# Scores of a banded attention as three products of split parts in place of one plain float32 product

## The chip, the cores and the metric

One Trainium2 chip, one core. The metric is the device time of one execution in microseconds; a kernel's time is the median of its runs.

## What is computed

The kernel computes two transformer-like blocks of two layers each, one after the other, on 256 tokens of width 1024. The change lies in the first block. Each of its layers has three branches: a state-space branch, a banded attention with rotated queries and keys (the one that changes), and a full attention with decay. Cut to the banded attention:

```python
def sliding_window_branch(q, k, v, z, sinks, cos, sin):
    q = rope(q.reshape(b, s, SWA_HEADS, HEAD_DIM), cos, sin)       # 16 heads of 64
    k = rope(k.reshape(b, s, SWA_KV_HEADS, HEAD_DIM), cos, sin)    # 4 heads of 64
    ...
    scores = einsum('bnqkgd,bnskd->bnkgqs', qb, kb) * HEAD_DIM ** -0.5   # blocks of 128, this block and the one before
    scores = where(band & (key_pos >= 0), scores, -inf)
    probs = softmax(concat([scores, sink], -1))[..., :-1]
    out = einsum('bnkgqs,bnskd->bnqkgd', probs, vb)
    return out.reshape(b, s, SWA_HEADS * HEAD_DIM) * silu(z)
```

All inputs are float32.

## The kernel before

Activations lie with features on the partitions and tokens on the columns. A dense unit (`dense`, line 287) multiplies 1024 by 256 weights with 256 tokens: 8 steps over the contraction, two blocks of 128 outputs, and three products each (`mm3`, line 245). Both operands are split: a rounded copy in float32r (ScalarE, `act`) and the rest (a VectorE or GpSimd subtraction, `tt`), and high x high, high x low and low x high are summed in PSUM. The weights come by DMA into `wr`, are copied to `wh` by ScalarE and their rest `wl` is made by VectorE, for one piece in four by GpSimd (`fetch`, line 115), for a unit two ahead of the one that is used.

The attention's own products (scores, transposes, probabilities times values) are plain float32 matmuls, with no split.

The order on TensorE is written out by hand: the program text is the order. Small work is woven between the dense units by a clock of its own: `spent` counts the columns streamed and calls `tick` every 3072, a half step; a dense unit is 2 steps. Tasks (`spawn`) are Python generators that yield the number of steps until they go on. A `Job` is one pair of heads: A makes scores and softmax, B, at least 2.5 steps later, the transposes, C the product with the values. The order on the other engines is made by the scheduler, which also inserts the waits.

In a layer of the first block, the banded attention comes after the full attention. First the keys' dense unit: ScalarE reads it out to `swk`, `rope` (line 775) starts four DMAs on ScalarE's queue that swap halves of 32 partitions into a scratch tile `s`, and a task follows: 2 steps later `s` is multiplied on GpSimd and the keys on VectorE, one step later VectorE adds the two. Then the values' unit. Then four rounds, one for each four query heads (loop at line 802): a dense unit for the queries, read out with the scale to `q`, `rope(q)`; a dense unit for the gate `z`; the two jobs are enqueued, 2 steps later at the earliest and after `turned` and `kturned` have ended; a dense unit for the merge gate and one that projects the other attention's output (`gate_proj`, line 758). `qk` (line 234) makes the scores: for the pair's two heads, which lie on partitions 0 to 63 and 64 to 127, first block by first keys (128 columns), then second block by all keys (256 columns). With 2 layers, 4 rounds and 2 pairs it runs 16 times for this attention, and as often for the full one, which keeps it.

Scratch tiles (`f2`, 2 KB a partition) come from a pool of 13 buffers in this block. In the trace all scratch tiles are named f, the scores' PSUM tiles ps, dense PSUM tiles pd, transposes pt, the product with the values po; line numbers are those of helpers (L92 `mm`, L98 `act`, L101 `tt`, L104 `stt`).

Of the kernel before, what the change touches and what calls it, by code (L numbers as in the profile page):

```python
# [6 lines left out]
F32 = mybir.dt.float32  # L7
F32R = mybir.dt.float32r
# [3 lines left out]
ALU = mybir.AluOpType  # L12
# [33 lines left out]
class Kern:  # L46
# [187 lines left out]
    def qk(self, pss, cuts, q, k):  # L234

        for a, b, c, d in cuts:
            for i, ps in enumerate(pss):
                p = slice(64 * i, 64 * i + 64)
                self.mm(ps[:, a:b], q[p, 128 * (a > 0):128 * (a > 0) + 128], k[p, c:d], True, True)

    def masked(self, out, ps, mask, least, init=3e38):

        self.V.tensor_tensor_reduce(out, ps, mask, 1.0, init, ALU.add, ALU.min, least)  # L243
# [266 lines left out]
def b1_layer(K, l, x, yr, sums, cw, wdt, first_sums=None):  # L510
# [112 lines left out]
    def gate_z(ps):  # L623
        zs = K.f2((128, 2, 256))
        K.act(zs, ps, AF.Tanh, scale=0.5)
        K.stt(zs, zs, 1.0, ps, ALU.add, ALU.mult)
        return zs
# [6 lines left out]
    def pv2(o, pair, v, pts):  # L634
        for i in range(2):
            K.mm(o[64 * i:64 * i + 64, pair, :], v(i, 0), pts[i][0], True, False)
        for i in range(2):
            K.mm(o[64 * i:64 * i + 64, pair, 128:256], v(i, 1), pts[i][1], False, True)

    def attn4(score, v, masks, mn_fix, done, wait=0, until=(), row0=None):  # L640


# [4 lines left out]
        def job(pair):  # L647
# [6 lines left out]
            def A():  # L654
                add = sh.get("b")
                mn = K.small([128, 2, 2], "mn")
                pss = [K.psx((128, 384)) for _ in range(2)]
                score(pair, pss)
                sh["p"] = prs = []
                if mn_fix is not None:  # L660
                    ns, sk = mn_fix(pair)
                for i, ps in enumerate(pss):
                    pr = add[i] if add else K.f2((128, 384))
                    for a, s in enumerate((slice(0, 128), slice(128, 384))):
                        K.masked(pr[:, s], ps[:, s], pr[:, s] if add else masks[a], mn[:, i, a:a + 1],
                                 3e38 if mn_fix is None else ns[:, i:i + 1])
                    prs.append(pr)
                den = K.small([128, 2, 2], "den")
                if mn_fix is not None:
                    es = K.small([128, 2, 2], "es")  # L670
                    K.tt(es, mn, sk, ALU.add)
                    K.act(es, es, AF.Exp)
                for i, pr in enumerate(prs):
                    for a, s in enumerate((slice(0, 128), slice(128, 384))):
                        K.act(pr[:, s], pr[:, s], AF.Exp, scale=-1.0, bias=mn[:, i, a:a + 1],
                              accum_out=den[:, i, a:a + 1])
                if mn_fix is not None:
                    K.tt(den, den, es, ALU.add)
                V.reciprocal(den, den)
                for i in range(2):  # L680
                    pr = prs[i]
                    V.tensor_scalar(pr[:, 0:128], pr[:, 0:128], den[:, i, 0:1], None, op0=ALU.mult)
                    V.tensor_scalar(pr[:, 128:384], pr[:, 128:384], den[:, i, 1:2], None, op0=ALU.mult)
# [27 lines left out]
    def gated(yt, zs, c0):  # L711
        def done(o):
            t = K.f2((128, 2, 256))
            K.stt(t, o, 0.5, zs, ALU.mult, ALU.mult)
            split_y(yt, t, c0)
        return done
# [4 lines left out]
    for i in range(4):  # L721
        q, kk, v = [K.f2((128, 2, 256)) for _ in range(3)]
        if i == 0:
            ps = K.dense(K.unit(), Hr, (0, 1))
# [23 lines left out]
        def score(pair, pss, q=q, kk=kk, i=i):  # L748
            K.qk(pss, ((0, 128, 0, 128), (128, 384, 0, 256)), q[:, pair, :], kk[:, pair, :])

        jc += attn4(score, lambda j, t, v=v: v[:, t, 64 * j:64 * j + 64], None, None, gated(yc, zs, 2 * i),
                    until=(steps,), row0=64 + 4 * i)

# [4 lines left out]
    def gate_proj(br, y, i, jobs, first):  # L758
        Y = (lambda k: y[:, 0, k, :], lambda k: y[:, 1, k, :])
        ps = K.dense(K.unit(), H, (0, 1))  # L760
        th = K.f2((128, 2, 256))
        for c in range(2):
            f = 8 * br + 2 * i + c
            K.act(th[:, c, :], ps[:, c, :], AF.Tanh, scale=0.5, bias=gbh[:, f:f + 1])
        K.finish_jobs(jobs)
        ps = K.dense(K.unit(), Y, (0, 1))
        m = merged[:, 2 * i:2 * i + 2, :]
        if first:
            K.stt(m, th, 1.0, ps, ALU.add, ALU.mult)
        else:  # L770
            K.stt(th, th, 1.0, ps, ALU.add, ALU.mult)
            K.tt(m, m, th, ALU.add, K.P)


    def rope(t):
        s = K.f2((128, 2, 256))
        for a in range(4):
            b = a ^ 1
            nc.scalar.dma_start(s[32 * a:32 * a + 32], t[32 * b:32 * b + 32])

        def task():
            yield 2
            K.tt(s, s, K.bc(K.rope[:, 1, :], 2), ALU.mult, K.P)
            K.tt(t, t, K.bc(K.rope[:, 0, :], 2), ALU.mult)
            yield 1
            K.tt(t, t, s, ALU.add)

        turned = K.spawn(task())
        K.step(turned)
        return turned  # L790

    ps = K.dense(K.unit(), H, (0, 1))
    kk = K.k_p.tile([128, 2, 256], F32, name="swk", tag="k0")
    K.act(kk, ps)
    kturned = rope(kk)
    ps = K.dense_tok(K.unit(), H)
    v = K.k_p.tile([128, 2, 256], F32, name="swv", tag="k1")
    K.act(v, ps)
    yb = K.r_p.tile([128, 2, NK, 256], F32R, name="yb", tag="r16")
    nsk = K.small([128, 16], "nsk")  # L800
# [1 line left out]
    for i in range(4):  # L802
        g0 = 2 * (i // 2)
        ps = K.dense(K.unit(), H, (0, 1))
        q = K.f2((128, 2, 256))
        K.act(q, ps, scale=-0.125)
        turned = rope(q)
        zs = gate_z(K.dense(K.unit(), H, (0, 1)))

        def score(pair, pss, q=q, i=i):  # L810
            K.qk(pss, ((0, 128, 0, 128), (128, 384, 0, 256)), q[:, pair, :], kk[:, i // 2, :])

        def fix(pair, i=i):
            s = slice(4 * i + 2 * pair, 4 * i + 2 * pair + 2)
            return (nsk[:, s],
                    vec("sink", 16 * l, 16)[:, s].unsqueeze(2).to_broadcast([128, 2, 2]))

        js = attn4(score, lambda j, t, g0=g0: v[:, t, 64 * (g0 + j % 2):64 * (g0 + j % 2) + 64],
                   (K.msk("u"), K.msk("le", 2)), fix, gated(yb, zs, 2 * i), 2, (turned, kturned))
        jb += js  # L820
        gate_proj(2, yc, i, jc, True)
# [92 lines left out]
    for i in range(4):  # L914
        ps = K.dense(K.unit(), H, (0, 1))
# [8 lines left out]
    for i in range(4):  # L924
        th = pend[i]
        w = K.unit()
        for cols in ((0,), (1,)) if i == 3 else ((0, 1),):
            ps = K.dense(w, Y, cols)
# [640 lines left out]
def program(tc, A, out, dbg=None):  # L1569
    with ExitStack() as ctx:  # L1570
# [14 lines left out]
        with ExitStack() as c1:  # L1585
# [49 lines left out]

            mods = K.spawn(later(), 5)
            mg = b1_layer(K, 0, x1, yr, sums, cw[0], wdt, first_sums)
            sums = K.sums_open(K.gather)
            yr = raw()
# [6 lines left out]

            b1_out(K, 0, x1, mg, sums, None, None, between)
            mg = b1_layer(K, 1, x1, yr, sums, cw[1], wdt)
            K.finish(mods)

# [297 lines left out]
```

## Time and profile before

| | us |
|---|---|
| median of 3 runs | 2063.96 |
| lowest and highest | 2060.04 and 2064.75 |
| the profiled execution's own time | 2062.68 |
| its span, first to last instruction | 2060.9 |
| TensorE matmuls busy | 2029.2 |
| VectorE, ScalarE, GpSimd busy | 1464.4, 991.1, 506.2 |

The profile is of one execution. PE is TensorE's matmul queue and PEld its weight loads, DVE is VectorE, ACT ScalarE, POOL GpSimd. Matmuls are pipelined: a row's duration reaches from the start of the first to the modelled end of the last, and so rows overlap; the distance between starts is what a matmul costs. float32r operands are shown as f32 in the matmuls' rows.

### The profile page before, as it was taken

The page shows a single profiled execution, that of the slowest core. Times are in us where ns is not written, and L with a number is a line of the kernel's source. Part 1 is how long each engine was busy: PE and PEld are TensorE (multiplying, and loading weights), DVE is VectorE, ACT ScalarE, POOL GpSimd, SP SyncE. Part 2 cuts the span into 40 slices and gives each one's busy share as a digit, 9 for nine tenths or more (in the row PEclk, how much of TensorE's full clock was granted, in tenths as well). Part 3 has the DMA queues.
Part 4 walks back from the last instruction along what each step waited for, and adds up shares of the span by engine and source line. Part 5 has one row for each costly group of instructions (what it writes and reads, how often), then busy time and mean ns, then how long its engine had stood idle before and what let it go on. Part 6 is the DMA issues. An engine that isn't in the chain of part 4 may idle for free.

```text
span 2060.9 us, 37605 instructions
## 1 busy us (share of the span) xinstructions
PE 2029.2 (98%) x14768; PEld 1839.0 (89%) x14768; DVE 1464.4 (71%) x2835; ACT 991.1 (48%) x2112; POOL 506.2 (25%) x393
## 2 busy tenths in 40 slices
PE   8999999999999999999999999999999999999998
PEld 7898999999898999999877888888888899999997
DVE  7777788976777788978466454865564576879984
ACT  6455555545455555555344333542332354556553
POOL 3232222324333123343100212111111121232222
PEclk9999999999999999999999999999999999999999
DMA  7765656665765656654111232232222233454552
GB/s 272 292 214 191 219 207 248 222 246 203 259 208 195 233 202 243 231 191 162 59 57 57 87 123 102 83 102 94 91 103 92 92 128 118 144 195 164 182 192 77
DMA packets 66304, 339.08 MB, mean 165 GB/s; under 512 B 7760, under 2 KB 22096, under 8 KB 29776
## 3 DMA queue, kind: packets, MB, share of 16 engines
q1 hardware_dynamic: 62000, 332.22, 45.7%
q10 hardware_dynamic: 4128, 4.46, 0.8%
q8 instruction: 116, 1.90, 0.4%
q14 instruction: 60, 0.49, 0.1%
HBM read 331.28 MB, written 1.44 MB: 161 GB/s over the span
## 4 chain that ended last, share of the span: by engine, by line
PE 92%; DVE 5%; issue 1%; ACT 1%; DMA 1%; SPq 0%; POOL 0%; DVEq 0%; POOLq 0%; ACTq 0%
PE pd L92 81%; PE ps L92 4%; PE po L92 3%; PE pt L92 2%; PE pt L95 2%; DVE wl L101 2%; DVE f L104 1%; DVE f L101 1%; ACT wh L98 0%; DMA wm<-in_wm_dram 0%; DVE h L104 0%; DMA x<-in_x_dram 0%; DVE f L984 0%; DVE hl L101 0%; ACT f L98 0%
## 5 line engine op out<-in xcount | busy, mean ns | idle before, releaser
L101 DVE TENSOR_TENSOR wl<-wr,wh 128x512 fp32r<-128x512 f32 x751 | 687.9, 934 | 244.7 <-ACT wh L98 243.1
L98 ACT ACTIVATE wh<-wr 128x512 fp32r<-128x512 f32 x992 | 561.2, 621 | 470.1 <-PE pd L92 262.1
L101 POOL TENSOR_TENSOR wl<-wr,wh 128x512 fp32r<-128x512 f32 x241 | 349.9, 1452 | 1238.9 <-ACT wh L98 1103.0
L92 PE MATMUL pd<-h,wh 128*128 128x256 f32 x2688 | 498.7, 286 | 2.4 <-ACT wh L98 1.4
L92 PEld LDWEIGHTS pd<-h,wh 128*128 128x128 f32 x2688 | 417.5, 191 | 26.4 <-issue 17.6
L92 PE MATMUL pd<-h,wl 128*128 128x256 f32 x1344 | 380.0, 283 | 0.7 <-DVE wl L101 0.7
L92 PE MATMUL pd<-hh,wh 128*128 128x512 f32 (+1 forms) x992 | 347.6, 350 | 1.5 <-ACT hh L98 1.5
L92 PE MATMUL pd<-hl,wh 128*128 128x512 f32 (+1 forms) x992 | 341.4, 344 | 3.7 <-DVE hl L101 3.7
L92 PE MATMUL pd<-hh,wl 128*128 128x512 f32 (+1 forms) x992 | 340.4, 343 | 0.0
L92 PEld LDWEIGHTS pd<-h,wl 128*128 128x128 f32 x1344 | 257.2, 191 | 1.2 <-DVE wl L101 0.9
L92 PEld LDWEIGHTS pd<-hh,wh 128*128 128x128 f32 x992 | 189.9, 191 | 30.4 <-issue 7.5
L92 PEld LDWEIGHTS pd<-hl,wh 128*128 128x128 f32 x992 | 190.1, 192 | 25.5 <-DVE hl L101 4.7
L92 PEld LDWEIGHTS pd<-hh,wl 128*128 128x128 f32 x992 | 190.0, 192 | 21.6
L92 PE MATMUL pd<-act,wh 128*128 128x256 f32 (+1 forms) x688 | 160.2, 327 | 0.0
L104 DVE SCALAR_TENSOR_TENSOR f<-pd,cw,f 128x255 f32<-128x255 f32 (+3 forms) x272 | 151.0, 555 | 11.0 <-ACT f L98 8.6
L92 PEld LDWEIGHTS pd<-act,wh 128*128 128x128 f32 x688 | 116.2, 190 | 11.1 <-DVE act L101 0.2
L92 PE MATMUL pd<-hf,wh 128*128 128x256 f32 x640 | 115.2, 283 | 0.0
L92 PE MATMUL pd<-mg,wh 128*128 128x256 f32 (+1 forms) x576 | 113.0, 296 | 0.1
L92 PE MATMUL pd<-act,wl 128*128 128x256 f32 (+1 forms) x344 | 112.2, 326 | 0.0
L98 ACT ACTIVATE f<-f,mn 128x128 f32<-128x128 f32 (+2 forms) x160 | 79.8, 500 | 46.8 <-DVE mn L243 46.6
L98 ACT ACTIVATE f<-pd,cw 128x256 f32<-128x256 f32 (+1 forms) x120 | 66.8, 557 | 69.6 <-DVE f L104 62.7
L92 PEld LDWEIGHTS pd<-hf,wh 128*128 128x128 f32 x640 | 99.8, 192 | 0.0
(257 smaller groups left out, 3216.5 us busy)
## 6 DMA issues: line engine op xcount, KB each, us to landing
wr<-in_w_dram SPq DMA_DIRECT2D x233, 1024.0 KB, 4.9
wm<-in_wm_dram SPq DMA_DIRECT2D x48, 1024.0 KB, 6.9
f<-far SPq DMA_DIRECT2D x32, 192.0 KB, 5.1
f<-far SPq DMA_DIRECT2D x24, 256.0 KB, 6.0
wr<-in_wd_dram SPq DMA_DIRECT2D x8, 768.0 KB, 4.2
wr<-in_wa_dram SPq DMA_DIRECT2D x8, 512.0 KB, 3.5
c<-in_c_dram SPq DMA_DIRECT2D x2, 1920.0 KB, 7.8
f<-f ACTq DMA_DIRECT2D x32, 64.0 KB, 2.0
```

Source lines behind the costliest of these rows:

```text
L92: self.T.matmul(out, l, r, start=start, stop=stop)
L95: self.T.transpose(out, in_, self.ident[0:k, 0:k])
L98: self.S.activation(out, in_, f, **kw)
L101: (eng or self.V).tensor_tensor(out, a, b, op=op)
L104: self.V.scalar_tensor_tensor(out, a, s, b, op0=op0, op1=op1)
```

## The change

`rope` is handed two tiles more. After the addition that ends the rotation, ScalarE copies the rotated tile to the first in float32r, and VectorE subtracts that copy from it into the second. The keys' two parts become `swk0` and `swk1` in the persistent buffers k0 and k1, the unsplit keys a scratch tile, and the values move to buffer k2. Each round's queries get two scratch tiles more. The scores are made by a new function `qk3`: for each of the two cuts three products, high x high, high x low, low x high, each for both heads in turn, summed in PSUM. Nothing else changes.

```diff
+    def qk3(self, pss, cuts, q, k):
+
+        (qh, ql), (kh, kl) = q, k
+        for a, b, c, d in cuts:
+            t = slice(128 * (a > 0), 128 * (a > 0) + 128)
+            for n, (x, y) in enumerate(((qh, kh), (qh, kl), (ql, kh))):
+                for i, ps in enumerate(pss):
+                    p = slice(64 * i, 64 * i + 64)
+                    self.mm(ps[:, a:b], x[p, t], y[p, c:d], n == 0, n == 2)
...
-    def rope(t):
+    def rope(t, parts):
...
             K.tt(t, t, s, ALU.add)
+            K.act(parts[0], t)
+            K.tt(parts[1], t, parts[0].bitcast(F32), ALU.subtract)
...
-    kk = K.k_p.tile([128, 2, 256], F32, name="swk", tag="k0")
-    K.act(kk, ps)
-    kturned = rope(kk)
+    kk = [K.k_p.tile([128, 2, 256], F32R, name="swk%d" % n, tag="k%d" % n) for n in range(2)]
+    kf = K.f2((128, 2, 256))
+    K.act(kf, ps)
+    kturned = rope(kf, kk)
     ps = K.dense_tok(K.unit(), H)
-    v = K.k_p.tile([128, 2, 256], F32, name="swv", tag="k1")
+    v = K.k_p.tile([128, 2, 256], F32, name="swv", tag="k2")
...
         K.act(q, ps, scale=-0.125)
-        turned = rope(q)
+        qs = [K.f2((128, 2, 256), F32R) for _ in range(2)]
+        turned = rope(q, qs)
...
-        def score(pair, pss, q=q, i=i):
-            K.qk(pss, ((0, 128, 0, 128), (128, 384, 0, 256)), q[:, pair, :], kk[:, i // 2, :])
+        def score(pair, pss, q=qs, i=i):
+            K.qk3(pss, ((0, 128, 0, 128), (128, 384, 0, 256)), [t[:, pair, :] for t in q],
+                 [t[:, i // 2, :] for t in kk])
```

## Rows read from the trace of the kernel before

**Rows 1.** The page: busy time by engine; the chain that ended last by engine.

```profile
PE 2029.2 (98%) x14768; PEld 1839.0 (89%) x14768; DVE 1464.4 (71%) x2835; ACT 991.1 (48%) x2112; POOL 506.2 (25%) x393
PE 92%; DVE 5%; issue 1%; ACT 1%; DMA 1%; SPq 0%; POOL 0%; DVEq 0%; POOLq 0%; ACTq 0%
```

**Rows 2.** Busy time by engine, both banded stretches together (139 to 275, 610 to 750).

```profile
sum 276.00, PE 274.65 PEld 248.03 DVE 207.23 ACT 150.88 POOL 70.98; mean PE 137.33 PEld 124.02 DVE 103.61 ACT 75.44 POOL 35.49
```

**Rows 3.** The banded scores by tile: count, duration in ns (min/median/max), starts, forms.

```profile
L92 PEld LDWEIGHTS ps<-swk,f x128: 182/188/188, 170.9 to 742.7; 64*128 64x128 f32 x128
L92 PE MATMUL ps<-swk,f x128: 272/375/378, 170.9 to 742.9; 64*128 64x128 f32 x64, 64*128 64x256 f32 x64
```

**Rows 4.** Timeline (start, us, engine, out<-in, count) of one unit, in narrow windows.

```profile
199.04 0.52 PEld L92 LDWEIGHTS ps<-swk,f 64*128 64x128 f32 x8
199.05 0.49 PE L92 MATMUL ps<-swk,f 64*128 64x128 f32 x4
199.37 0.60 PE L92 MATMUL ps<-swk,f 64*128 64x256 f32 x4
199.90 0.38 PE L92 MATMUL pd<-yc,wh 128*128 128x256 f32 x1
```

**Rows 5.** Timeline of TensorE inside a dense unit.

```profile
198.24 0.40 PE L92 MATMUL pd<-h,wh 128*128 128x256 f32 x2
198.48 0.28 PE L92 MATMUL pd<-h,wl 128*128 128x256 f32 x1
```

**Rows 6.** Timeline of all engines where an attention output is split.

```profile
150.54 0.68 DVE L104 SCALAR_TENSOR_TENSOR f<-po,f 128x512 f32<-128x512 f32 x1
...
151.25 0.63 ACT L98 ACTIVATE yc<-f 128x512 fp32r<-128x512 f32 x1 [3.12 <-DVE f L104]
...
151.92 0.69 DVE L101 TENSOR_TENSOR yc<-f,yc 128x512 fp32r<-128x512 f32 x1
```

**Rows 7.** Timeline of VectorE, second round of layer 0: product, addition, what follows.

```profile
191.71 1.76 DVE L101 TENSOR_TENSOR f<-f,rope 128x512 f32<-128x512 f32 x1
...
198.09 0.68 DVE L101 TENSOR_TENSOR f<-f,f 128x512 f32<-128x512 f32 x1
199.75 0.69 DVE L101 TENSOR_TENSOR wl<-wr,wh 128x512 fp32r<-128x512 f32 x1 [0.98 <-ACT wh L98]
```

**Rows 8.** Timeline of five more rounds: the addition, then the round's first scores.

```profile
228.01 0.68 DVE L101 TENSOR_TENSOR f<-f,f 128x512 f32<-128x512 f32 x1
...
229.13 0.93 PE L92 MATMUL ps<-swk,f 64*128 64x128 f32 x8
...
258.14 0.68 DVE L101 TENSOR_TENSOR f<-f,f 128x512 f32<-128x512 f32 x1
...
259.18 0.93 PE L92 MATMUL ps<-swk,f 64*128 64x128 f32 x8
...
670.16 0.68 DVE L101 TENSOR_TENSOR f<-f,f 128x512 f32<-128x512 f32 x1
...
673.33 0.93 PE L92 MATMUL ps<-swk,f 64*128 64x128 f32 x8
...
700.58 0.68 DVE L101 TENSOR_TENSOR f<-f,f 128x512 f32<-128x512 f32 x1
...
701.37 0.93 PE L92 MATMUL ps<-swk,f 64*128 64x128 f32 x8
...
730.33 0.68 DVE L101 TENSOR_TENSOR f<-f,f 128x512 f32<-128x512 f32 x1
...
731.45 0.93 PE L92 MATMUL ps<-swk,f 64*128 64x128 f32 x8
```

**Rows 9.** Timeline of ScalarE, second round of layer 0: its next weight copies.

```profile
199.09 2.19 ACT L98 ACTIVATE wh<-wr 128x512 fp32r<-128x512 f32 x4 [2.05 <-PE pd L92]
```

**Rows 10.** Timeline in layer 1: the keys' addition; the transposes that TensorE waits to start.

```profile
620.41 0.69 DVE L101 TENSOR_TENSOR swk<-swk,f 128x512 f32<-128x512 f32 x1 [1.82 <-POOL f L101]
...
622.56 0.97 PE L95 MATMUL pt<-cst,f 128*128 128x128 f32 x6 [1.35 <-DVE f L683]
```

## Prediction

> **What bounds the kernel now.** I read the page's engine line and chain first [rows 1]: TensorE's matmuls are busy 98% of the span and carry 92% of the chain of work that ended last, while VectorE is busy 71% and ScalarE 48%. So work saved on TensorE comes back one for one, and work given to the other engines is free as long as no matmul waits for it. Then the busy time of the two stretches that hold the banded attention (136 us in layer 0, 140 us in layer 1) [rows 2]: 274.7 of 276.0 us on TensorE, 207.2 on VectorE, 150.9 on ScalarE. TensorE has no gap there to hide anything in. Last the timelines around the scores, for which order on which engine decides what the matmuls wait for.
>
> **The scores on TensorE.** The group of the scores' matmuls counts 128 [rows 3]. The program has 2 layers x 4 rounds x 2 pairs x 2 cuts x 2 heads = 64, so each plain float32 product is issued as two instructions. One unit (one call for one pair: 8 instructions, 16 units in all) can be taken apart [rows 3, 4]. The two heads use different halves of the rows and start together: 8 weight loads of 0.19 fit in 0.52 us, so four pairs of loads stand 0.11 us apart ((0.52 - 0.19) / 3). The pairs of matmuls start at 199.05, 199.27 (0.49 - 0.27 later), 199.37 and 199.59 (0.60 - 0.38 later), and the next dense matmul at 199.90. Read as steps: first load 0.11, two narrow halves (128 columns) of 0.11, two wide ones (256) of 0.22, and a tail of 0.09 until the array turns to the next shape. Sum 0.86 (0.85 between the rows' starts).
>
> After the change a unit is 12 products with one instruction each, as the dense units have it, in six pairs: three narrow, three wide. A wide one: the dense 128x256 product of rounded parts has a pitch of 0.12 (two take 0.40, one 0.28) [rows 5]. A narrow product of rounded parts does not occur in this trace, so it is bounded. From below 0.06, half a wide one, if only columns count. From above 0.22, the two halves that a plain narrow product takes, if the rounded format gains nothing on so few columns. I take 0.11: each product needs its own weight load, and loads of exactly this shape stand 0.11 apart [rows 4]; that is the nearest row. A unit is then 0.11 + 3 x 0.11 + 3 x 0.12 + 0.09 = 0.89, against 0.86: +0.03, over 16 units **+0.5 us** (bounds: 0.74 gives -1.9, 1.22 gives +5.8). The half pass that three products save against four is eaten by the loads of the narrow ones.
>
> The rows put the narrow pace at the load's 0.11. The Trainium skill, page "TensorE: Matmul & The Clock Gate", section "LDWEIGHTS (loading the stationary operand)", says the same against this change: a load costs its 128 columns however few rows it has. The section "Back-to-back issue gap" of that page also has an isolated gap of N/2.4 + 2.5 ns, 56 ns for 128 columns, which leaves the load out and by which, as an estimate, the units would save some 2 us in place of adding 0.5; it warns itself that this counts too little for small N.
>
> **The split of the queries.** Each round of four heads gets a ScalarE copy to rounded form and a VectorE subtraction behind the rope's last addition, on queries that the next scores need. The same three steps stand in the trace where an output is split: VectorE ends at 150.54 + 0.68 = 151.22, ScalarE copies from 151.25 for 0.63, VectorE subtracts from 151.92 for 0.69 and ends at 152.61 [rows 6]. So the low part is there 1.39 us after the addition; with 0.03 to TensorE, 1.42. The high part is there after 0.69.
>
> Is there that much room? In the second round of layer 0 the addition stands behind a queue on VectorE: it runs 198.09 to 198.77, though the product before it ended at 191.71 + 1.76 = 193.47 [rows 7]. The scores start at 199.05 [rows 4], right after the tail of the dense unit, so nothing is waited for now, but the room is 0.28 us. The other rounds, addition's end to the scores [rows 8]: 0.44 and 0.36 in layer 0; 2.49, 0.11 and 0.44 in layer 1. The first rounds have several us, as their scores queue behind the other attention's jobs. TensorE's order is written out by hand, so a late part holds everything behind the scores: the next dense unit and the weight splits that wait for its buffers.
>
> The low queries are the third of the six pairs, whose load would start 0.22 after the first. The stall is 1.42 - 0.22 - room = 1.20 - room: 0.92, 0.76 and 0.84 in layer 0, none at room 2.49, 1.09 and 0.76 in layer 1: **+4.4 us**. For this the new steps must run at once. ScalarE is idle there, its next weight copies start at 199.09 after 2.05 idle [rows 9], and VectorE is idle for 0.98 until 199.75 [rows 7]; there is the place, if the scheduler's order puts the copy ahead of those four weight copies (2.19 us) and the subtraction ahead of their subtractions.
>
> **The split of the keys.** One per layer, needed by the first scores, two dense units later. In layer 1 the keys' addition (620.41, ends 621.10) stands directly ahead of VectorE's normalisation of the other attention, for which TensorE waits already: 1.35 us at 622.56 [rows 10]. A subtraction that waits for its copy in between adds up to 1.4; placed behind, nothing. Neither is nearer, so I take the middle, **+0.7 us**. In layer 0 no matmul waits at that place.
>
> **The rest.** Ten copies and ten subtractions are 10 x 0.63 = 6.3 us of ScalarE and 10 x 0.69 = 6.9 us of VectorE. In the stretches of [rows 2] VectorE has 276 - 207 = 69 us to spare and weights are fetched two units ahead; I cost it at nothing beyond the stalls, and up to 2 us if a weight's low part comes late. The pool of scratch tiles has 13 buffers; a round took 13 and takes 15. Counting what is alive at one time I get at most 13, so I cost it at nothing; a missing buffer would hold a read-out, a few us. The values move to another buffer (k2), and the swap DMAs stay four per rope from the unsplit tile: nothing. Later stages are untouched.
>
> Sum: +0.5 + 4.4 + 0.7 = **+5.6 us**. The profiled execution took 2062.7 (span 2060.9), 1.3 below the median of the runs shown, 2064.0. On the one it gives 2068.3, on the other 2069.6; I say 2069.0, and work the rivals from the mean of the two, 2063.3.
>
> **The rivals.**
> Narrow products at full price: if a rounded product with 128 columns takes what a plain one does (0.22), units cost +5.8 and the low queries are wanted 0.2 later, so 1.0 of stall goes: +5.8 + 3.4 + 0.7 = 9.9, 2073. For it: no dense product here has fewer than 256 columns, so nothing shows the gain. Against it: the dense pitch goes by columns.
> The split falls behind the weights: if the copy stands after the four weight copies in ScalarE's queue, it starts at 201.3 in the second round in place of 198.8; the stall grows by 2.5, in five rounds 12.5, and some 1 more in the sixth: +19, 2082. For it: VectorE already runs the keys' addition ahead of steps that were written earlier, so the order is not that of the program. Against it: the split of an output keeps its place ahead of the weights.
> **Not slower:** the addition moves up in VectorE's queue. Its operands are ready at 193.47 and it waits 4.6 us behind other VectorE work [rows 7]. If the scheduler, seeing two more steps behind it, lets it end 1.2 us or more ahead of the scores (two instructions of 0.6 earlier), the 4.4 are gone: +1.2, 2064.5. Against it: nothing in the change raises its priority.
> Columns alone set the narrow pace: units give back 1.9 and the stalls stay: -1.9 + 4.4 + 0.7 = 3.2, 2066.5. This is the isolated gap of the page named above; against it stand the loads' 0.11.
>
> **How the numbers follow.** Forecast 0.44, full price 0.18, behind the weights 0.13, addition moves up 0.15, columns alone 0.10. What a measurement of this kernel can tell from no change is about 0.2%, 4.1 us: 2059.8 to 2068.1. The forecast lies just above that edge and I give two thirds of it to slower (0.30); with 0.17 of full price and all 0.13 of the third that is 0.60. Within 0.2% fall the rest of the forecast, the two cheap rivals and a little of full price: 0.37 less what their scatter sends below, so 0.36 same and 0.04 faster. The range takes in all but the far end of the split behind the weights and the lower scatter of the cheap rivals: 2063 to 2078.
>
> **What would show it.** In the profile after: 96 narrow and 96 wide matmuls of the scores, with starts of narrow pairs 0.11 apart (0.06 or 0.22 else) and about 0.89 from a free unit's start to the next work; TensorE waiting, at five scores, 0.4 to 0.6 for a ScalarE copy and then again for a VectorE subtraction, 0.8 to 1.1 together; VectorE and ScalarE some 7 and 6 us busier. A stall above 2 us there would mean the split behind the weights. No waits at the scores with VectorE's addition earlier would mean that it moved up, and the forecast is wrong by its largest term.

## The result and the profile after

The kernel after takes 2079.98 us (median of 6 runs, 2075.93 to 2082.09) against 2063.72 for the kernel before on the same chip: a ratio of 1.0077, with a 95% interval of 1.0062 to 1.0092. It is slower by 16 us, beyond the range that ended at 2078. The profiled execution took 2080.85, 18.2 more than that of before. The page's engine line and the chain, answering to [rows 1]:

```profile
PE 2038.9 (98%) x14832; PEld 1848.5 (89%) x14832; DVE 1468.4 (71%) x2845; ACT 997.7 (48%) x2122; POOL 506.8 (24%) x393
...
PE 86%; DVE 8%; DMA 2%; issue 2%; ACT 2%; ACTq 0%; POOL 0%; SPq 0%; DVEq 0%; POOLq 0%
```

VectorE and ScalarE are busier by 4.0 and 6.6 us (the ten subtractions and ten copies were put at 6.9 and 6.3), and neither is near its limit. But the chain that was 92% TensorE is 86%, and VectorE and DMA took the rest. The same two stretches as in [rows 2], and the scores by tile as in [rows 3]:

```profile
sum 276.00, PE 266.62 PEld 242.66 DVE 201.85 ACT 149.08 POOL 72.56; mean PE 133.31 PEld 121.33 DVE 100.93 ACT 74.54 POOL 36.28
```

```profile
L92 PEld LDWEIGHTS ps<-swk,f x192: 182/186/188, 173.1 to 758.7; 64*128 64x128 f32 x192
L92 PE MATMUL ps<-swk,f x192: 269/277/332, 173.1 to 758.8; 64*128 64x128 f32 x96, 64*128 64x256 f32 x96
```

TensorE, which had 1.4 us free in 276, now has 9.4. What it waited for in the banded stretches (engine, line, releaser: us in total, times, longest):

```profile
PE pt L95 <- DVE f L693: 4.1, 1, 4.1
PE ps L92 <- ACT f L98: 3.2, 4, 0.9
PE ps L92 <- DVE f L101: 1.4, 5, 0.3
```

The two waits of the scores (ps) were in the forecast. The first line, one wait of the keys' transposes, was 1.35 us before [rows 10].

**At the scores.** Timeline of the third round of layer 0 in the kernel after (start, us, engine, out<-in, count, idle time before and its releaser), with a free unit from the round's second pair behind it:

```profile
232.24 0.68 DVE L101 TENSOR_TENSOR f<-f,f 128x512 f32<-128x512 f32 x1
...
232.96 0.63 ACT L98 ACTIVATE f<-f 128x512 fp32r<-128x512 f32 x1 [1.77 <-DVE f L101]
233.49 2.18 ACT L98 ACTIVATE wh<-wr 128x512 fp32r<-128x512 f32 x4
233.62 0.69 DVE L101 TENSOR_TENSOR f<-f,f 128x512 fp32r<-128x512 f32 x1 [0.70 <-ACT f L98]
...
233.64 0.44 PE L92 MATMUL ps<-swk,f 64*128 64x128 f32 x4 [0.95 <-ACT f L98]
...
234.37 0.73 PE L92 MATMUL ps<-swk,f 64*128 64x128 f32 x8 [0.29 <-DVE f L101]
...
245.06 0.95 PE L92 MATMUL ps<-swk,f 64*128 64x128 f32 x12
245.95 0.51 PE L92 MATMUL pd<-h,wh 128*128 128x256 f32 x2
```

The addition ends at 232.92, the high part at 233.59, the low part at 234.31, and TensorE takes it at 234.37, 1.45 after the addition (forecast: 1.42). The copy stands ahead of the four weight copies. A unit that waits for nothing takes 0.89 (245.06 to 245.95), as worked out.

**At the keys of layer 1.** Timeline of the kernel after, all engines (ACTq and SPq are issues of transfers):

```profile
616.51 0.58 ACT L98 ACTIVATE f<-pd 128x512 f32<-128x512 f32 x1
...
616.99 1.66 ACT L98 ACTIVATE wh<-wr 128x512 fp32r<-128x512 f32 x3
...
617.42 1.52 PE L92 MATMUL po<-f,f 128*64 128x256 f32 x16
...
618.38 2.44 ACTq L789 DMA_DIRECT2D f<-f  x4
...
620.14 13.79 SPq L123 DMA_DIRECT2D wr<-in_w_dram  x2
...
627.23 0.69 DVE L101 TENSOR_TENSOR f<-f,rope 128x512 f32<-128x512 f32 x1 [4.84 <-DMA f<-f]
...
629.07 1.73 DVE L101 TENSOR_TENSOR f<-f,f 128x512 f32<-128x512 f32 x1 [1.07 <-POOL f L101]
...
630.73 0.28 DVE L692 TENSOR_SCALAR f<-f,den 128x128 f32<-128x128 f32 x1
...
631.26 1.51 PE L95 MATMUL pt<-cst,f 128*128 128x128 f32 x6 [4.08 <-DVE f L693]
```

The same place before, where the read-out is at 610.55:

```profile
610.55 0.58 ACT L98 ACTIVATE swk<-pd 128x512 f32<-128x512 f32 x1
...
611.16 2.45 ACTq L779 DMA_DIRECT2D f<-swk  x4
...
616.81 1.78 DVE L101 TENSOR_TENSOR swk<-swk,rope 128x512 f32<-128x512 f32 x1
...
618.07 7.16 SPq L123 DMA_DIRECT2D wr<-in_w_dram  x2
```

Before, the swap was issued as soon as the read-out ended, and the next weight transfer left 4.5 us after the issue of its four was over. Now it is issued 1.29 us after the read-out's end (617.09), and the weight transfer, 1 MB, leaves at 620.14, just ahead of the last of the four (620.21). Two transfers of 192 KB (from 618.97 and 619.45) run beside it too. The swap's data is there only at 627.2. VectorE works in order: the keys' product has its place ahead of the other attention's normalisation (630.73), so VectorE sits idle for 4.84 us, and TensorE waits for the normalisation. The new copy and subtraction stand in no part of this wait. How long the swaps took from issue to landing, over all 40, first of before and then of after:

```profile
DMA to landing us min/median/max: 1.9/2.0/5.7
```

```profile
DMA to landing us min/median/max: 1.9/2.1/7.0
```

**At the swaps of the tight rounds.** The second to fourth rounds of a layer are the tight ones, as their scores follow the rotation closely. From the first issue of a swap to its last landing these six took 3.85 to 4.1 us before. After, five of the six take longer: 5.6 and 5.1 in the third and fourth rounds of layer 0, and 5.3, 4.6 and 4.6 in layer 1. In the last two no weight transfer runs beside the swap. What all five have inside is one packet of 16 KB on the queue that the page calls instruction (its line for the kernel after):

```profile
q8 instruction: 117, 1.92, 0.4%
```

Before, none of its 116 packets falls into one of these six swaps. In the last two rounds the packet comes during the issues, and these take longer as well: 3.16 us on ScalarE's queue in the third round of layer 1 (2.44 before), so that ScalarE's next weight copy starts 3.81 us after the start of the read-out in place of 3.10.

```profile
700.03 3.16 ACTq L789 DMA_DIRECT2D f<-f  x4
...
703.24 1.16 ACT L98 ACTIVATE wh<-wr 128x512 fp32r<-128x512 f32 x2 [2.71 <-issue]
```

The other kernels with swaps agree: in those with plain scores (the kernel before, its three variants and the split alone of the next section) no such packet falls into a tight swap, and these take 3.8 to 4.2 us; with the products of parts most have one inside. No experiment moved the packets alone.

**The clock.** Busy time in four stretches of the kernel after (stretch, length, PE, PEld, DVE, ACT, POOL, then the granted clock as a share of full speed, DMA share and GB/s):

```profile
625.00:632.00 7.00, 2.92 (x23) 2.74 (x22) 3.71 (x8) 2.64 (x5) 2.99 (x2) 0.84 0.08 31
...
632.00:636.00 4.00, 4.00 (x20) 3.02 (x19) 3.71 (x13) 1.60 (x6) 0.00 (x0) 0.50 0.38 84
...
710.00:714.00 4.00, 3.07 (x26) 2.72 (x25) 3.30 (x6) 1.76 (x4) 0.00 (x0) 1.00 0.47 137
...
714.00:718.00 4.00, 3.71 (x24) 3.24 (x28) 3.46 (x13) 3.85 (x15) 1.38 (x1) 0.64 0.31 131
```

Around the end of the wait for the keys the granted clock is 0.50, which is 1.2 GHz, for 6.8 us in all (from 629.8, still within the wait), and behind a stall at the scores (713.56) for 3.4 us. In the kernel before no stretch between 600 and 770 is below 1.00.

**The account.** From the starts of the same matmuls in both traces, the 18.2 us between the two profiled executions come to:

| | forecast, us | measured, us |
|---|---|---|
| scores on TensorE, 16 units | +0.5 | +0.5 |
| stalls at the first scores of the rounds | +4.4 | +6.3 |
| wait at the keys' transposes, layer 1 | +0.7 | +2.6 |
| half clock behind that wait | 0 | +2.3 |
| half clock behind the stall at 714 | 0 | +1.5 |
| two waits around the first round of layer 0 | 0 | +1.3 |
| one wait in the second block (1036) | 0 | +1.2 |
| start of the execution, ahead of any changed instruction | 0 | +1.4 |
| not assigned | 0 | +1.1 |

### The profile page after: what moved, and what is told of

It reads as the page before. It is cut to its first block, busy times and chain, and to the rows that moved or that the text cites. A ratio compares the mean times of both kernels' runs of the same rounds, so it can differ in the third digit from the quotient of the medians.

```text
span 2078.9 us, 37773 instructions
## 1 busy us (share of the span) xinstructions
PE 2038.9 (98%) x14832; PEld 1848.5 (89%) x14832; DVE 1468.4 (71%) x2845; ACT 997.7 (48%) x2122; POOL 506.8 (24%) x393
## 4 chain that ended last, share of the span: by engine, by line
PE 86%; DVE 8%; DMA 2%; issue 2%; ACT 2%; ACTq 0%; POOL 0%; SPq 0%; DVEq 0%; POOLq 0%
PE pd L92 76%; PE ps L92 4%; DVE wl L101 3%; PE po L92 2%; PE pt L92 2%; PE pt L95 2%; DVE f L101 1%; DVE f L104 1%; ACT wh L98 1%; ACT f L98 1%; DMA wr<-in_w_dram 1%; DMA f<-f 0%; DVE h L104 0%; DVE f L999 0%; ACTq L1067 0%
```

## The experiments

The theory when these runs were planned was that the split's steps cost only what they make the scores wait, and that the rest comes of transfers that land late with VectorE in order behind them. Rivals: the added instructions themselves; a missing scratch buffer. Each ratio is against runs of the kernel before on the same chip.

### Which part costs

**The split made but not read**: the scores stay plain products of the unsplit tiles, and the keys' unsplit tile gets a buffer of its own.

```diff
-    kf = K.f2((128, 2, 256))
+    kf = K.k_p.tile([128, 2, 256], F32, name="swf", tag="k3")
...
-            K.qk3(pss, ..., [t[:, pair, :] for t in q], [t[:, i // 2, :] for t in kk])
+            K.qk(pss, ..., q[:, pair, :], kf[:, i // 2, :])
```

> The splits are made, the scores stay plain float32 products of the unsplit queries and keys; the unsplit keys lie in a persistent buffer of their own (k3), not in the scratch pool; nobody reads the parts. Late parts (the stall at the scores is the cost): nothing waits for a split, so 0 to +2 us against the kernel before. Scratch pool (the unsplit keys and the two tiles more a round are the cost): the keys' share is gone and the queries' parts are freed at once, so also 0 to +2. If the added ScalarE and VectorE work itself is the cost, +5 or more.

2067.9 us, 1.0032 (1.0019 to 1.0046). No score waits and no product of parts is left, yet 5.6 us remain, as much as the expectation gave to the added work itself; the run without swaps below speaks against that. What TensorE waits for in the trace is another place, 3.1 us at the product with the values of the other attention, behind a swap that took 9.3 us. The traced execution was the fastest of the seven (2063.53), so its waits don't explain the median.

**The parts made of the tiles before the rotation**, so that the scores don't wait for the rotation's end:

```diff
+        K.act(parts[0], t)
+        K.tt(parts[1], t, parts[0].bitcast(F32), ALU.subtract)
...
             K.tt(t, t, s, ALU.add)
-            K.act(parts[0], t)
-            K.tt(parts[1], t, parts[0].bitcast(F32), ALU.subtract)
```

> Changed kernel, but the parts are split from the queries and keys before the rotation, as soon as they are read out; the rotation is still worked out and its result left unused. Counts, tiles and products are those of the changed kernel; only the parts are there some 10 us before the scores. Late parts: the 6.3 us of waits at the scores and 1.5 us at half clock behind one of them go: about +8 us against before in place of +16. Scratch pool alone: unchanged, +16.

2071.89, 1.0045 (1.0033 to 1.0057): no wait at the scores, but 2.9 at the keys' transposes and 2.7 at the values' product.

**The scores' jobs half a step later**, all work kept:

```diff
             K.tt(parts[1], t, parts[0].bitcast(F32), ALU.subtract)
+            yield 1.5
```

> Changed kernel, but a round's jobs start half a step (3072 streamed columns, some 1.9 us of TensorE's work at least) later than the split's last instruction is written. Late parts: the waits at the scores go as the split has that much more room, about +8 us against before. Scratch pool: the parts are held longer, so +16 or a little more.

2072.13, 1.0044 (1.0032 to 1.0056), 9.8 above the kernel before, where the kernel after is 16.3 above. The waits at the scores are gone, and 6.5 us with them: the 6.3 of the stalls and the 1.5 of the clock behind one of them, less 1.2 by which the keys' wait grew (to 5.3). The half clock behind that wait stays (6.8 us from 628). In the trace the scores of the tight rounds come 2.7 to 5.1 us later after their swap than in the kernel before, so the edit gave more room than its half step of 1.9 us.

The same half step in the kernel before:

> Kernel before, with no split, its jobs half a step later. If only the split's lateness and order cost, the same as before within 1.5 us. If the later jobs themselves cost (scratch tiles held longer, other order), some of the 9 us that stay when the jobs of the changed kernel start later are seen here.

2064.55, 1.0011 (1.0002 to 1.0020): the later jobs by themselves cost at most 4 us, so what is left of the 9.8 is mostly the keys.

### The scratch buffers

**The keys' unsplit tile in a buffer of its own** (the first line of the first diff, alone):

> Changed kernel, but the unsplit keys lie in the persistent buffer k3, which is free then, and not in the scratch pool. Scratch pool: the 4.9 us lost ahead of the transposes in layer 1 (wait and half clock) and up to 1.3 us of late read-outs in layer 0 go: about +10 us against before. Late parts alone: the stalls at the scores stay and so do the 4.9, +16. Order and transfers (the swap of the keys landed late because a weight transfer was issued into it): anything from +10 to +16, as the order changes with the tile.

2077.79, 1.0075 (1.0062 to 1.0088). The keys' wait falls to 0.7, as their swap is again issued right behind its read-out (615.04, read-out's end 615.01). So the scratch pool does matter there. In the kernel after and in all seven variants that keep the swaps and the keys in a scratch tile, the swap leaves 0.9 to 1.0 us after the start of a values' product (617.42 and 618.38 above); in the others it leaves 0.3 ahead of that product. So its issue waits for TensorE there: it writes into a tile whose buffer this product still reads. But the time is that of the kernel after, as the loss moved to the next swap:

```profile
633.25 1.19 SPq L468 DMA_DIRECT2D wm<-in_wm_dram  x2
633.46 2.47 ACTq L789 DMA_DIRECT2D f<-f  x4
...
644.00 0.69 DVE L101 TENSOR_TENSOR f<-f,rope 128x512 f32<-128x512 f32 x1 [5.43 <-DMA f<-f]
...
644.60 0.55 DVE L703 COPY f<-pt 128x384 f32<-128x384 f32 x1
...
645.21 0.87 PE L92 MATMUL po<-f,f 128*64 128x256 f32 x8 [3.78 <-DVE f L703]
```

Two transfers of 1 MB leave just ahead of the queries' swap and within it; its last part lands 8.6 us after its issue, VectorE waits 5.43, and the read-out that TensorE needs stands behind.

**All new tiles outside the pool**, so that a round takes 13 scratch tiles again; then the same with the jobs half a step later:

```diff
+    kf = K.k_p.tile([128, 2, 256], F32, name="swf", tag="k3")
...
+        qs = [K.k_p.tile([128, 2, 256], F32R, name="swh", tag="k3"),
+              K.sm1_p.tile([128, 2, 256], F32R, name="swl", tag="rows")]
```

> Changed kernel, but the unsplit keys and both parts of the queries lie in persistent buffers that are free then (k3, and the one of the rows), so that a round takes 13 scratch tiles as before the change. Scratch pool: the 4.9 us at the transposes of layer 1 and up to 1.3 of late read-outs in layer 0 go and nothing comes back later, about +9 us against before. Transfers (the swap of the rotation lands late where a weight transfer runs beside it, and VectorE, in order, holds the read-outs behind it): the losses in layer 1 stay, at one place or another, +13 to +17.

> e6 with the jobs half a step later. Late parts and scratch pool together are all: +1 us or less against before (the units' +0.5). Transfers: the scores wait no more, but 5 to 9 us stay in layer 1 ahead of transposes or the product with the values.

2078.12, 1.0076 (1.0064 to 1.0089), and 2071.73, 1.0047 (1.0034 to 1.0059): no better than with the tiles in the pool. The pool decides where the loss falls, not how large it is.

### The transfers

**No swap transfers** (the products read the unswapped tile; the rotation is left incomplete):

```diff
-        for a in range(4):
-            b = a ^ 1
-            nc.scalar.dma_start(s[32 * a:32 * a + 32], t[32 * b:32 * b + 32])
...
-            K.tt(s, s, K.bc(K.rope[:, 1, :], 2), ALU.mult, K.P)
+            K.tt(s, t, K.bc(K.rope[:, 1, :], 2), ALU.mult, K.P)
```

> Changed kernel without the swap of halves by DMA: the rotation multiplies the unswapped tile on GpSimd, so that the four transfers a rope and their waits are left out of the computation; all else as changed. Transfers: the waits at the scores fall to at most the 4.4 us that the rooms of the kernel before gave, or vanish, as the addition comes earlier; the 4.9 in layer 1 go: 0 to +6 us against before. Scratch pool: still +10 or more, as the tiles are the same.

2062.79, 1.0004 (0.9995 to 1.0013). With every new copy, subtraction and product in place, the whole loss is gone, the stalls at the scores too. So the loss hangs on the swaps, and the added work without them costs little. How little is not shown to the microsecond: the wait of 1.35 us that the kernel before has at the keys goes too, and that kernel was not run without swaps.

**More time for the swap.** The products 3 steps after the issue in place of 2, with the wait of 1.5 steps of the half-step run kept; the same with the tiles outside the pool; and the products' step alone in the kernel before:

```diff
-            yield 2
+            yield 3
```

> The changed kernel with two numbers of its rotation task altered: the swapped halves are multiplied 3 steps after the swap is issued instead of 2, and the scores' jobs start a half step later. Theory A (the loss is VectorE and GpSimd standing in order behind swap transfers that land up to 7 us after their issue): with one step, some 7 us, more for the swap, the waits of 3 to 5 us in layer 1 (keys' transposes, first round's values product) and the stretch at half clock behind them go, and no score waits; the kernel is 0.5 to 2 us above the one before, about what the run without the swap gave. Theory B (the loss is the added instructions themselves, wherever the products stand): the waits of layer 1 stay, and the time is that of the jobs-half-later run, about 9 us above the kernel before. Theory C: a third step only moves the wait, as the later products stand in front of other VectorE work: 4 to 9 us above.

> The same two numbers altered (products 3 steps after the swap, jobs a half step later), and the keys' unsplit tile and the queries' two parts in buffers of their own, so that a round takes 13 scratch tiles again. Theory A (transfers): no different from the run with the two numbers alone, to 1 us. If a missing scratch buffer costs anything once the transfers have time, this one is 2 us or more faster than that.

> The kernel before with one number altered: the products 3 steps after the swap is issued instead of 2. Theory A: the keys' wait of 1.35 us before layer 1's transposes goes, and nothing else waits, as the scores then have a step less room but still come after the sum: 0 to 1.5 us faster than before. Theory C: the rotation's sum comes a step later, and the scores wait for it in some rounds: 1 to 5 us slower.

2100.11, 1.0191 (1.0178 to 1.0205); 2099.04, 1.0180 (1.0166 to 1.0194); 2062.63, 1.0003 (0.9994 to 1.0012). The first two are far off every expectation. A step is some 3.8 us, not 7 (a round of 30.1 us has 8), and these two put off the jobs by more than half a step: their task ends 5.5 steps after the issue, that of the half-step run 4.5. Waits of the first:

```profile
PE pt L95 <- ACT f L98: 8.9, 2, 4.5
PE pt L95 <- DVE f L692: 8.5, 5, 2.0
PE pt L95 <- DVE f L693: 4.3, 1, 4.3
```

The jobs now come due so late that a round's end orders their transposes right behind the softmax, and TensorE waits there seven times (first two lines): the experiment added a loss of its own. And the keys' wait stays at 4.3; in the kernel before it stays at 1.5. So two more kernels, one with half a step after the split, so that the jobs come as late as in the half-step run, and one with the step alone:

> The changed kernel with the swapped halves multiplied 3 steps after the swap is issued instead of 2, and a half step between the split and the scores' jobs. The jobs then come due as late as in the run with the jobs half a step later (4.5 steps after the swap is issued); only the products differ from that run. Theory A (VectorE stands in order behind swaps that land late): the layer-1 waits of 3 to 5 us at the keys' transposes and the half-clock stretch go; 0.5 to 3 us above the kernel before. Theory B (the lateness of the transfers is not it): as that run, about 9 us above. Theory C (any later order piles up the jobs at the end of the round): waits at the transposes after each round's scores, 10 us or more above.

> The changed kernel with one number altered: the products 3 steps after the swap is issued instead of 2, and the jobs a step later by that alone. Theory A: the layer-1 keys' wait and its half-clock stretch go, the waits at the scores (1.2 less the room, up to 6 us together) stay, as the split still ends where the jobs come due: 4 to 9 us above the kernel before. Theory C: 10 us or more above, with waits at the transposes after the scores.

2070.00, 1.0046 (1.0032 to 1.0060), and 2082.25, 1.0097 (1.0081 to 1.0112). A later product doesn't help. In the first, VectorE has it in the same place, ahead of the normalisation, and idles for 5.02 us: the task's step says when an instruction is written, not where VectorE's order puts it. My "more time for the swap" gave it none.

**The swap on the queue of the weights:**

```diff
-            nc.scalar.dma_start(s[32 * a:32 * a + 32], t[32 * b:32 * b + 32])
+            nc.sync.dma_start(s[32 * a:32 * a + 32], t[32 * b:32 * b + 32])
```

> The changed kernel with the four swap transfers of a rotation issued by SyncE, on the queue of the weights, in place of ScalarE's. Theory A: where a swap lands 4 to 9 us after its issue it is because a weight transfer of 1 MB shares the 16 engines with it. On one queue it stands either ahead of the weights and lands in 2 to 3 us, or behind a whole weight transfer and lands later still, and the waits follow: if ahead, layer 1's waits go and the time is 3 to 8 us under the changed kernel's; if behind, more waits, and slower than the changed kernel by some us. Rival: the landing has nothing to do with the weights, and neither the landing times nor the time change by more than 2 us.

2066.72, 1.0024 (1.0013 to 1.0034): 4.5 us above the kernel before in place of 16.3, so 11.8 less by this one word. The place of the keys:

```profile
616.29 1.52 PE L92 MATMUL po<-f,f 128*64 128x256 f32 x16
...
617.22 2.42 SPq L789 DMA_DIRECT2D f<-f  x4
...
620.87 9.06 SPq L123 DMA_DIRECT2D wr<-in_w_dram  x2
...
622.42 0.35 DVE L693 TENSOR_SCALAR f<-f,den 128x256 f32<-128x256 f32 x1
...
623.14 0.68 DVE L101 TENSOR_TENSOR f<-f,rope 128x512 f32<-128x512 f32 x1
```

```profile
DMA to landing us min/median/max: 1.9/2.0/4.1
```

The swap still waits for its buffer, but SyncE issues in order, so all four stand ahead of the weight transfer, and no part of a swap takes more than 4.1 us from its issue. The normalisation now stands ahead of the product on VectorE, the transposes (625.88) wait for nothing, and the clock is 1.00 from 622 to 636. The earlier landing and the new order came together; this run doesn't part them. The word changes a third thing: the issue of a swap, 2.4 us, no longer stands among ScalarE's work.

At the scores the same trace says more. Third and fourth rounds of layer 0, VectorE's addition and the first scores:

```profile
226.63 1.77 DVE L101 TENSOR_TENSOR f<-f,f 128x512 f32<-128x512 f32 x1 [1.17 <-POOL f L101]
...
232.05 0.44 PE L92 MATMUL ps<-swk,f 64*128 64x128 f32 x4
...
261.91 0.68 DVE L101 TENSOR_TENSOR f<-f,f 128x512 f32<-128x512 f32 x1
...
263.30 0.44 PE L92 MATMUL ps<-swk,f 64*128 64x128 f32 x4 [0.69 <-ACT f L98]
```

The swaps of these two rounds still take 5.1 and 5.4 us (5.6 and 5.1 in the kernel after). But in the third the addition now stands directly behind the products and ends 8.9 us after the swap's first issue (12.8 in the kernel after), and the scores start without a wait (0.18 for the low part). So it is in five of the six tight rounds (6.6 to 8.9; 12.1 to 12.8 in the kernel after). In the fourth round the old order stands (12.6), and TensorE waits. By this trace most of the stalls at the scores went with VectorE's new order, and not because the swaps landed sooner.

The Trainium skill, page "DMA: Bandwidth & Descriptors", section "Issuing engines are not separate DMA queues", says that transfers of all issuing engines interleave on the same 16 DMA engines, and that more issuers save only the time of issuing. The 7.0 us beside a transfer of another queue agree with the first part; no run here shows the time of issuing apart from the order.

**Queue and half step together, and the queue in the kernel before:**

> The changed kernel with the swap transfers on SyncE's queue, the weights', and the scores' jobs a half step later. If the loss is the landing of the swaps plus the waits at the scores, both are gone and the time is 0.5 us (units) to 3 us above the kernel before. If something else came with the change, it stays at 4 to 5 us above, like the run with the queue alone.

> The kernel before with its swap transfers on SyncE's queue, the weights'. If the landing of the swap costs the kernel before little (one wait of 1.35 us before layer 1's transposes), this is 0 to 2 us faster than before; if the weights queue behind a swap that waits for its read-out, up to 5 us slower. Faster by more than 3 us would mean that the queue, and no part of the change, explains what the run with the queue gained on the changed kernel.

2064.49, 1.0007 (0.9999 to 1.0016), and 2064.58, 1.0005 (0.9996 to 1.0014). With both, the change costs 1.4 us (-0.2 to 3.3), and from 130 to 780 the longest wait of TensorE is 0.7, one between the banded stretches that the kernel before has too. Its tight swaps of layer 1 still take 4.3 to 5.1 us, each with an instruction packet inside, and TensorE waits for none of them:

```profile
PE ps L92 <- DVE f L104: 0.7, 1, 0.7
PE pt L95 <- DVE f L604: 0.6, 1, 0.6
```

The kernel before gains nothing by the queue, though its wait of 1.35 us at the keys goes. No version here beats it.

## Why the forecast was wrong in size and right in sign

The forecast was +5.6 us; the kernels differ by 16.3 (medians) and the two traces by 18.2. Three steps of the sum failed: the room at the scores, the cost of the keys' split, and the swaps and the clock at nothing.

**The units: right.** 0.89 each and +0.5 in all, with 96 narrow and 96 wide products. The rivals that priced the narrow product at 0.22 or 0.06 fall: the pace is the load's. The isolated gap of the Trainium skill's page "TensorE: Matmul & The Clock Gate" would have saved 2 us; the section on loads, by which the 128 columns count, agrees: a load of 64 rows takes 0.19 us here, one of 128 rows 0.19 too.

**The queries' split: mechanism right, term too small** (6.3 in place of 4.4). The chain took 1.45 in place of 1.42, at once, ahead of the weight copies, so the rival of the split behind the weights is refuted, though its 2082 lies near the result. What failed is "the room": I took it from the trace of before as if the addition kept its distance to the scores. In the third round of layer 0 it was 0.44 there [rows 8]; after, TensorE could have begun at 232.69 (233.64 - 0.95), 0.23 before the addition's end. The product there waits 0.64 for the swap, which it didn't before, so the addition came some 0.7 later and the stall was 1.5. The last two rounds of layer 1 lost 1.5 each (forecast: 1.09 and 0.76). There the product did not wait for the swap's data; the longer issue held ScalarE's weight copies, and with them VectorE's work up to the addition, by 0.7. The addition did not move up here; with the swaps on the weights' queue it did, and most of the stalls went, as that rival said.

**The keys: wrong.** The step "a subtraction that waits for its copy in between adds up to 1.4; placed behind, nothing" looked at the new instructions alone. They cost nothing there. The wait grew because the unsplit keys had become a scratch tile: the swap found its buffer in use, left 1.3 us later, and met the weight transfer and two smaller ones. The upper bound of that term held no transfer.

**The rest at nothing: wrong in two places.** "The swap DMAs stay four per rope ...: nothing" counted them and didn't ask when each leaves and beside what. And "a missing buffer would hold a read-out" named the right resource and the wrong victim: it held a transfer. The granted clock was in no term; its two half-speed stretches give 3.8 us.

**Open.** The wait of 1.2 us in the second block lies on instructions that the change doesn't touch. It goes with the instruction packets as well: in the 13 kernels that have it (0.9 to 1.4 us) such a packet lies within the swap that starts 16 to 18 us ahead of it, and that swap takes 6.7 to 7.4 us; in the other five (0.2 to 0.6) none does, and it takes 5.9 to 6.3. These five are the kernels with plain scores. That the added products shift the packets in time is the likeliest reading, but it is argued and not shown; nor is it shown whose instructions they are. Open too is how the 11.8 us of the queue divide between earlier landing, VectorE's order and a ScalarE that doesn't issue.

## What to carry to other kernels

A copy and a subtraction put behind an operation that ends just in time cost their latency less the room, and the room itself moves when something upstream does; price it from the transfer's issue, not from the last addition, and look what follows the issue on the engine that makes it. When a persistent tile becomes a scratch tile, look which transfer takes the next buffer and what it will meet on the DMA engines. A small transfer that an in-order engine waits for is worth issuing ahead of the large ones. One queue for both had that effect here, but it also gave VectorE another order, so read the trace for which of the two paid.

## What the runs showed of the hardware

A swap transfer of 64 KB that lands in 2.0 us in the median took 7.0 with a weight transfer of 1 MB issued just ahead of its last part (two transfers of 192 KB and an instruction packet ran too), and up to 8.6 beside two of 1 MB and an instruction packet. In the tight rounds, swaps without an instruction packet took 3.85 to 4.1 us in the kernel before, and those with one well inside 4.6 to 5.6 in the kernel after; a packet of 16 KB that came during the issues went with issues of 3.2 us in place of 2.4. The granted clock was 1.2 GHz for 6.8 us from within a matmul wait of 4.1 us, and for 3.4 us behind stalls of about 1.5 us (at 714) and of 3.8 us (keys in a buffer of their own): a wait of TensorE here cost up to about twice its length. The stall of 1.5 in the third round of layer 0 was followed by no such stretch (clock 1.00 from 234 to 242).
